# Half of the gated head outputs turned by transposing transfers instead of TensorE

## The chip, the cores and the metric

The kernel runs on one core of a Trainium2 chip. The metric is the device time of one execution in microseconds (us), as the median of several runs. In the tables PE is TensorE, PEld its weight loads, DVE is VectorE, ACT ScalarE, POOL GpSimd, and SP the SyncE queue that issues most loads. A tile has 128 partitions (P = 128).

## The reference

One decoder layer works on 512 tokens of 1024 channels in float32. Its two token mixers stand side by side: a convolution module, and a gated linear attention with four heads of 256 output channels. The change lies at the end of the attention:

```python
o = _gla_chunked(qh, kh, vh, gkh)                       # (1, 512, 4 heads, 256)
o = o * lax.rsqrt(jnp.mean(o * o, axis=-1, keepdims=True) + EPS) * gla_norm_g[l]
o = o.reshape(bsz, seq, GLA_VDIM) * jax.nn.silu(r)      # r is a product of the layer's input
y_gla = o @ w_gla_out[l]                                # (512, 1024) @ (1024, 1024)
merged = jax.nn.sigmoid(gate_a) * y_conv + jax.nn.sigmoid(gate_b) * y_gla
h = h + merged @ w_o[l]
```

A gated feed-forward block and a last normalization follow. The result is the (512, 1024) output.

## The kernel before

All large products are split into high and low parts: a float32 operand is copied on ACT into a rounded high part (`hi`), DVE subtracts it from the original to give the low part (`lo`), and `mm3` (L537 to L543) adds three products, low by high, high by low, high by high. So each weight tile of 128 x 1024 passes SP (load into `raw`), ACT (cast to `whi`) and DVE (subtract to `wlo`) ahead of PE. `split_weight` (L414) does that two weights ahead of the product that uses them (`LOOK = 2`).

A planner puts the instructions of each engine and of SP's queue in an order by their readiness and their place in the program text; each engine then works through its own list in order. `tc.issue_after(x)` pins what stands in its block behind `x` on the same engine.

The attention leaves its normalized outputs in `ot[p, n]`: token tile p (0 to 3, 128 tokens on partitions), column half n (512 of the 1024 channels). The product with `w_r` runs next, as a seven-product scheme over 2 x 2 blocks (`seven`, L1453). Its blocks come out in the order (token tiles 0 and 1, n = 0), (0 and 1, n = 1), (2 and 3, n = 1), (2 and 3, n = 0). `put_r` (L1544) evicts them into `rt[t, n]`, takes the SiLU on ACT, and lets DVE multiply the block finished before into `ot` (L1561); the last one is multiplied at L1565.

The product with `w_gla` needs channels on partitions. `gated_o(m)` (L1246) turns channel tile m (128 channels): four TensorE transposes (L1250), one for each token tile, into one PSUM bank of 512 tokens, which ACT scales by the norm's gain into the high part (L1257), and from which DVE makes the low part (L1258); the pair is `oa[m]`. Channel tiles 4 to 7 come from n = 1 and 0 to 3 from n = 0. `r_at` calls it for 4 and 5 during the last step of `w_r`. `pair_7(0)` calls it for 6, 7, then 0, 1, then 2, 3 after the first three of the four parts of its product pair with `w_gb` (`two_tiles`, L1344: parts x1, x3, x2, x4, each of some 24 products of 256 columns). Behind that pair stand the `w_gla` tiles 0 and 1 on PE, which read `oa[0]` to `oa[7]` in order, and then the pairs with `w_ga`.

In `two_tiles` a bank that a product adds to again is first copied out by ACT (`put`, L1351). POOL makes sums of weights (L398), pinned behind the instructions in `behind`.

Of the kernel before, what the change touches and what calls it, by code (L numbers as in the profile page):

```python
# [10 lines left out]
F32 = mybir.dt.float32  # L11
F32R = mybir.dt.float32r
BF16 = mybir.dt.bfloat16
U8 = mybir.dt.uint8
AF = mybir.ActivationFunctionType
ALU = mybir.AluOpType

P = 128
# [82 lines left out]
def trunk_layer(ctx: ExitStack, tc: tile.TileContext, a: dict, out: bass.AP):  # L101
    nc = tc.nc

    def pool(name, bufs, space=None):
        kw = {"space": space} if space is not None else {}
        return ctx.enter_context(tc.tile_pool(name=name, bufs=bufs, **kw))
# [9 lines left out]
    up = pool("acts", 1)  # L116
    tp = pool("temps", 1)
    ps = pool("psum", 1, bass.MemoryType.PSUM)
    edge = ctx.enter_context(tc.tile_pool(name="edge", bufs=1, side="right"))
    heap_scope, hp = scoped("heap", 26)  # L120
    conv_scope, vp = scoped("conv", 10)
# [5 lines left out]
    def nm(s):  # L127
        return f"{s}_{next(names)}"

    def heap(dt=F32):  # L130
        return hp.tile([P, T], dt, tag="h", name=nm("h"))
# [144 lines left out]
    pair_raws = {}  # L276
    kept = {}
    used = [0]
    pace = [None]

    def load():
        if len(raws) < len(order):
# [131 lines left out]
    def split_weight(halves=False, between=None):  # L414

        if len(ready) < len(order):
            while len(raws) <= len(ready):
                load()
            raw = raws[len(ready)]
            name, spec = order[len(ready)]  # L420
            if name in SEVEN or name == "two":
                raw = operand(raw, *spec) if name in SEVEN else two_operand(*spec)
                n = raw.shape[-1]
                hi = wp.tile([P, D], F32R, tag="whi", name=nm("whi"), bufs=4)[:, :n]
                lo = wp.tile([P, D], F32R, tag="wlo", name=nm("wlo"), bufs=4)[:, :n]
                nc.scalar.copy(hi, raw)  # L426
                two_low[:] = [nc.vector.tensor_tensor(lo, raw, hi.bitcast(F32), ALU.subtract)]  # L427
                with ExitStack() as order_of:
                    for ins in behind:
                        order_of.enter_context(tc.issue_after(ins.ins))  # L430
                    sum_on(name, *spec) if name in SEVEN else two_sums(*spec)
                ready.append((hi, lo))
                refill()
                return
            hi = wp.tile([P, D], F32R, tag="whi", name=nm("whi"), bufs=4)
            if order[len(ready)][0] == "w_low":
                nc.scalar.copy(hi, raw)
                if order[len(ready)][1] == 0:
                    part_lo = lambda t: t.rearrange("p (k c) -> p k c", c=P)[:, :, :RANK]
# [16 lines left out]
            nc.scalar.copy(hi, raw)  # L456
            if (name, spec) in ADDED:
                pace[0] = nc.scalar.mul(lo, raw, -1.0)  # L458
                nc.gpsimd.dma_start(lo, a[name][spec], accum_op=ALU.add)
            elif (name, spec) in POOLED:  # L460
                for c in (slice(0, T), slice(T, D)):
                    pace[0] = nc.gpsimd.tensor_tensor(lo[:, c], raw[:, c], hi[:, c].bitcast(F32), ALU.subtract)
            else:
                pace[0] = nc.vector.tensor_tensor(lo, raw, hi.bitcast(F32), ALU.subtract)  # L464
            ready.append((hi, lo))
            refill()

# [775 lines left out]

    ot = {}

    def gated_o(m, bank):  # L1246
        po = bank()
        c = (m % 4) * P
        for p in range(NT):
            nc.tensor.transpose(po[:, p * P : (p + 1) * P], ot[p, m // 4][:, c : c + P], ident)  # L1250
        gain = pp[:, PP_GG + m % 2 : PP_GG + m % 2 + 1]
# [4 lines left out]
        hi, lo = (both[:, 0, :], both[:, 1, :]) if m < 4 else (heap(F32R), heap(F32R))  # L1256
        nc.scalar.activation(hi, po, AF.Copy, scale=gain)  # L1257
        low_at[:] = [nc.vector.scalar_tensor_tensor(lo, po, gain, hi.bitcast(F32), ALU.mult, ALU.subtract)]  # L1258
        oa[m] = hi, lo

    part = [None] * KT

# [79 lines left out]
    combined = []  # L1342

    def two_tiles(name, p, q, acts7, side_bank, at_once=False):  # L1344

        x, y, z = mm_bank(), side_bank(), side_bank()
        c1, c2 = tmp(), tmp()
        t1, t2 = slice(0, H), slice(H, T)

        def put(c, acc):  # L1350
            nc.scalar.copy(c, acc[:, :H])  # L1351

        def combine(c, l, r, op):
            combined[:] = [nc.vector.tensor_tensor(c, l, r, op)]
# [185 lines left out]
    def sums_for(step):  # L1540
        while urgent and step in ("s1", "n2", "s4", "n3") and step not in merge_acts:
            urgent.pop(0)[1]()

    def put_r(step, t, n, acc):  # L1544
        if step in ("a11", "s1", "n2"):
            rt[t, n] = rp_.tile([P, T], F32, tag="r", name=nm("r"), bufs=6)
            return nc.scalar.copy(rt[t, n], acc)
        if step == "a22":
            rt[t, n] = rp_.tile([P, T], F32, tag="r", name=nm("r"), bufs=6)
            nc.scalar.activation(rt[t, n], acc, AF.Silu)  # L1550
        else:
            r = rt[t, n]
            one, two = (r, acc) if step == "n3" else (acc, r)
            done = nc.vector.tensor_tensor(r, one, two, ALU.add if step == "a12" else ALU.subtract)
            nc.scalar.activation(r, r, AF.Silu)
        if step == "a22":
            done = None
        with tc.issue_after(done.ins) if done else ExitStack():
            while gated:
                i, j = gated.pop()  # L1560
                nc.vector.tensor_tensor(ot[i, j], ot[i, j], rt[i, j], ALU.mult)  # L1561
        gated.append((t, n))
        if (step, t, n) == ("a22", 3, 0):
            i, j = gated.pop()
            nc.vector.tensor_tensor(ot[i, j], ot[i, j], rt[i, j], ALU.mult)  # L1565
        return done if step == "n3" else None

    def r_at(step, i):
        if (step, i) == ("a22", 1):
            for m in range(4, 6):  # L1570
                gated_o(m, ax_bank)

    seven("w_r", R_PAIRS, [ByTile(k) for k in range(4)], None, r_at, put=put_r, before=sums_for)
    half_of = [range(KT // 2), range(KT // 2, KT)]
    open_tiles = {}

# [2 lines left out]
    def pair_7(n):  # L1579
# [5 lines left out]
        for j in range(4):  # L1585
# [4 lines left out]
                while len(after) > 1:  # L1590
                    fill(1)
            if n == 0 and j < 3:
                for m in ((6, 7), (0, 1), (2, 3))[j]:
                    gated_o(m, ax_bank)
                if j == 2:
                    start_norms()
            if j == 0 or n >= 2:
# [424 lines left out]
```

## Time and profile before

| what | value |
|---|---|
| median of 3 runs | 817.36 us (817.26 to 817.85) |
| the profiled execution, its own time | 816.96 us |
| its span | 815.3 us |
| PE busy | 807.5 us (99%) |
| DVE busy | 700.7 us (86%) |
| ACT busy | 487.9 us (60%) |
| transposes of L1250 | 32, first at 284.2 us, last at 296.2 us |

The span is the time from the first to the last instruction that the profile shows; the execution's own time is 1.7 us longer. In the timeline a row has the start, the duration, the engine, the line, the operation with its tiles, and in brackets the idle time before it with what ended it. PE's matmuls overlap, so what one costs in the stream is read from the starts, not from its duration. Tiles carry the name of their buffers: `h` is the heap, `oa` the pair of channel tiles 0 to 3, `ax`, `mm` and `cv` are PSUM banks.

### The profile page before, as it was taken

To read this page: it belongs to the slowest core of one execution; us is meant where nothing else is said; L and a number is where in the kernel's file an instruction comes from. 1 tells how busy PE (TensorE), PEld (TensorE's weight loads), DVE (VectorE), ACT (ScalarE), POOL (GpSimd) and SP (SyncE) were. 2 spreads that over 40 slices of the span, in tenths; PEclk is the share of its full clock that TensorE was granted. 3 is DMA by queue.
4 is the path that set the end of the run, shared out by engine and by line. 5 is a ranking of instruction groups with operands and counts; after the bars stand their busy time and mean duration, and the time that the engine had idled before them with its cause. 6 is when DMAs were issued, how large, how long until landed. Compare 5 with 4: busy or idle time off the path is not lost.

```text
span 815.3 us, 11441 instructions
## 1 busy us (share of the span) xinstructions
PE 807.5 (99%) x4215; PEld 693.2 (85%) x4215; DVE 700.7 (86%) x1108; ACT 487.9 (60%) x746; POOL 192.5 (24%) x166
## 2 busy tenths in 40 slices
PE   9999999999999999999999999999999999999996
PEld 7888888788888898989888898898889988899885
DVE  6679999998998988486779899979976999789896
ACT  6667788677546575494435655556435663466655
POOL 2025433332204332122001100320133300522010
PEclk9999999999999999999999999999999999999999
DMA  8487858745831232432458613145732345334662
GB/s 337 146 198 179 187 160 176 161 119 135 186 95 60 78 130 78 137 105 95 164 124 220 190 57 126 52 154 156 144 127 92 142 117 167 105 104 171 165 129 105
DMA packets 36616, 113.60 MB, mean 139 GB/s; under 512 B 3704, under 2 KB 8960, under 8 KB 36560
## 3 DMA queue, kind: packets, MB, share of 16 engines
q1 hardware_dynamic: 29200, 86.92, 30.8%
q0 software_dynamic: 7200, 25.69, 18.0%
q8 instruction: 33, 0.54, 0.3%
q14 instruction: 23, 0.19, 0.1%
q10 hardware_dynamic: 160, 0.27, 0.1%
HBM read 110.76 MB, written 2.10 MB: 138 GB/s over the span
## 4 chain that ended last, share of the span: by engine, by line
PE 84%; DVE 13%; issue 1%; ACT 1%; DMA 1%; SPq 0%; DVEq 0%; ACTq 0%
PE mm L541 20%; PE mm L542 20%; PE mm L543 20%; DVE c L902 5%; PE cv L541 4%; PE cv L542 4%; PE cv L543 4%; DVE aside L902 3%; PE ax L542 2%; PE ax L541 2%; PE ax L543 2%; PE ax L1230 1%; PE ax L1232 1%; DMA kept<-in_w_r_dram 1%; PE ax L1212 0%
## 5 line engine op out<-in xcount | busy, mean ns | idle before, releaser
L541 PE MATMUL mm<-uh,wlo 128*128 128x512 f32 (+1 forms) x532 | 193.9, 364 | 0.2 <-DVE wlo L464 0.2
L542 PE MATMUL mm<-ul,whi 128*128 128x512 f32 (+1 forms) x532 | 191.6, 360 | 0.0
L543 PE MATMUL mm<-uh,whi 128*128 128x512 f32 (+1 forms) x532 | 191.4, 360 | 0.0
L427 DVE TENSOR_TENSOR wlo<-raw,whi 128x1024 fp32r<-128x1024 f32 x82 | 96.0, 1178 | 36.0 <-ACT whi L426 32.2
L398 POOL TENSOR_TENSOR raw<-raw,raw 128x512 f32<-128x512 f32 x39 | 63.9, 1638 | 236.3 <-DVE wlo L427 130.9
L541 PEld LDWEIGHTS mm<-uh,wlo 128*128 128x128 f32 x532 | 100.5, 189 | 15.6 <-DVE wlo L464 0.6
L543 PEld LDWEIGHTS mm<-uh,whi 128*128 128x128 f32 x532 | 100.4, 189 | 15.4
L542 PEld LDWEIGHTS mm<-ul,whi 128*128 128x128 f32 x532 | 100.5, 189 | 14.7
L426 ACT CAST whi<-raw 128x1024 fp32r<-128x1024 f32 x82 | 78.9, 965 | 41.4 <-PE mm L543 24.4
L456 ACT CAST whi<-raw 128x1024 fp32r<-128x1024 f32 x80 | 83.5, 1048 | 27.5 <-PE mm L543 13.9
L464 DVE TENSOR_TENSOR wlo<-raw,whi 128x1024 fp32r<-128x1024 f32 x50 | 66.3, 1331 | 7.1 <-ACT whi L456 6.8
L426 ACT CAST whi<-kept 128x1024 fp32r<-128x1024 f32 (+1 forms) x40 | 40.1, 1008 | 32.4 <-DVE kept L374 16.5
L902 DVE SCALAR_TENSOR_TENSOR aside<-cv,pp,aside 128x255 f32<-128x255 f32 (+6 forms) x112 | 52.2, 466 | 0.0
L902 DVE SCALAR_TENSOR_TENSOR c<-aside,btmp,c 128x247 f32<-128x247 f32 (+13 forms) x93 | 52.1, 565 | 0.0
L427 DVE TENSOR_TENSOR wlo<-kept,whi 128x1024 fp32r<-128x1024 f32 (+1 forms) x40 | 47.5, 1191 | 4.9 <-ACT whi L426 4.7
L902 DVE SCALAR_TENSOR_TENSOR c<-cv,pp,c 128x247 f32<-128x247 f32 (+13 forms) x93 | 43.2, 465 | 1.4 <-ACT c L898 1.4
L458 ACT ACTIVATE wlo<-raw 128x1024 fp32r<-128x1024 f32 x28 | 29.4, 1059 | 19.1 <-PE mm L541 19.1
L1351 ACT COPY tmp<-mm 128x256 f32<-128x256 f32 x38 | 14.1, 370 | 35.1 <-PE mm L543 34.3
L1733 DVE SCALAR_TENSOR_TENSOR tmp<-mm,pp,tmp 128x511 f32<-128x511 f32 (+1 forms) x42 | 31.2, 743 | 3.5 <-ACT tmp L1730 3.4
L1733 DVE SCALAR_TENSOR_TENSOR tmp<-tmp,pp,tmp 128x511 f32<-128x511 f32 (+1 forms) x32 | 27.8, 888 | 0.3
L1504 DVE TENSOR_TENSOR hres<-hres,mm 128x512 f32<-128x512 f32 (+1 forms) x37 | 24.7, 676 | 2.2 <-PE mm L543 2.1
L542 PE MATMUL cv<-ul,whi 128*128 128x512 f32 (+1 forms) x72 | 25.6, 356 | 0.0
(514 smaller groups left out, 2078.3 us busy)
## 6 DMA issues: line engine op xcount, KB each, us to landing
raw<-in_w_up_dram SPq DMA_DIRECT2D x44, 512.0 KB, 3.2
raw<-in_w_glu_dram SPq DMA_DIRECT2D x16, 512.0 KB, 5.1
raw<-in_w_down_dram SPq DMA_DIRECT2D x16, 512.0 KB, 3.4
wlo<-in_w_glu_dram POOLq DMA_DIRECT2D x12, 512.0 KB, 7.1
kept<-in_w_down_dram POOLq DMA_DIRECT2D x9, 512.0 KB, 5.5
raw<-in_w_v_dram SPq DMA_DIRECT2D x8, 512.0 KB, 6.0
raw<-in_w_qk_dram SPq DMA_DIRECT2D x8, 512.0 KB, 6.3
raw<-in_w_gb_dram SPq DMA_DIRECT2D x8, 512.0 KB, 4.0
```

The source lines that it names most:

```text
L398: work = nc.gpsimd.tensor_tensor(out, x, y, ALU.add)
L426: nc.scalar.copy(hi, raw)
L427: two_low[:] = [nc.vector.tensor_tensor(lo, raw, hi.bitcast(F32), ALU.subtract)]
L456: nc.scalar.copy(hi, raw)
L458: pace[0] = nc.scalar.mul(lo, raw, -1.0)
L464: pace[0] = nc.vector.tensor_tensor(lo, raw, hi.bitcast(F32), ALU.subtract)
L541: nc.tensor.matmul(acc, ll, rh, start=first, stop=False, **kw)
L542: nc.tensor.matmul(acc, lh, rl, start=False, stop=False, **kw)
L543: nc.tensor.matmul(acc, lh, rh, start=False, stop=last, **kw)
L902: nc.vector.scalar_tensor_tensor(out[:, j:], x[:, : half_t - j], w, out[:, j:], ALU.mult, ALU.add)
L1504: done = nc.vector.tensor_tensor(hres[t, n][:, c], hres[t, n][:, c], acc[:, c], op)
L1733: nc.vector.scalar_tensor_tensor(z[:, s:], acc[:, : T - s], w[j], z[:, s:], ALU.mult, ALU.add)
```

## The change

Token tiles 0 and 1 are turned by transfers, tiles 2 and 3 still by TensorE. After a block of tile 0 or 1 is gated, `words` has ACT reorder its float32 values into two planes of 16-bit words (all low words of a token, then all high ones), in the buffer of the SiLU tile that is no longer used, and SP writes them to DRAM, two rows for each token. When both tiles of a column half are written, `turn_o(n)` reads them back by transposing transfers, so that channels lie on partitions and the two words of a value beside each other again: one transfer of 512 rows by 512 words for n = 0, two of 512 by 256 for n = 1.

`gated_two` takes two channel tiles: for each two transposes into a bank of its own, and the high and low parts in halves of 256 tokens (`half_o`): the lower half from the landed tile, the upper one from the bank. The order on ACT and DVE is pinned: lower halves of 0 to 3 behind the last `put`, upper halves behind the last SiLU, lower halves of 4 to 7 behind the upper halves of 0 to 3, the next splits of `w_ga` and of `w_gla` tile 2 behind these, and the splits of `w_gb` behind the last reordering.

```diff
+    def words(t, n):
+        planes = rt[t, n].bitcast(U16).rearrange("p (two c) -> p two c", two=2)
+        behind_planes[:] = [nc.scalar.copy(planes, ot[t, n].bitcast(U16).rearrange("p (c two) -> p two c", two=2))]
+        rows = words_of[n][2 * t * P : 2 * (t + 1) * P, :]
+        nc.sync.dma_start(rows.rearrange("(p two) c -> p two c", two=2), planes)
+
+    def turn_o(n):
+        if n == 0:
+            landings = [rp_.tile([P, 4, H], F32, tag="rx", name=nm("turned"), bufs=1)]
+        else:
+            landings = [rp_.tile([P, 2, H], F32, tag="r", name=nm("turned"), bufs=6) for _ in range(2)]
+        many = 4 // len(landings)
+        for i, landing in enumerate(landings):
+            c = slice(i * many * P, (i + 1) * many * P)
+            nc.sync.dma_start(landing.bitcast(U16), words_of[n][:, c], transpose=True)
+            for j in range(many):
+                turned[4 * n + i * many + j] = landing[:, j, :]
+
+    def gated_two(m, bank):
+        for j in range(2):
+            po, c = bank(), (m % 4 + j) * P
+            for p in (2, 3):
+                nc.tensor.transpose(po[:, (p - 2) * P : (p - 1) * P], ot[p, m // 4][:, c : c + P], ident)
+            start_o(m + j)
+            if m < 4:
+                half_o(m + j, slice(0, H), turned[m + j], copied, ())
+            late_halves[:] = half_o(m + j, slice(H, T), po[:, :H], last_silu, ())
+        if m < 4:
+            low_at[:] = late_halves[1:]
+            for j in range(2):
+                behind_halves[:] = half_o(m + 4 + j, slice(0, H), turned[m + 4 + j], late_halves[:1], late_halves[1:])
+
+    def half_o(m, c, x, behind_high, behind_low):
+        (hi, lo), gain = oa[m], pp[:, PP_GG + m % 2 : PP_GG + m % 2 + 1]
+        with following(behind_high):
+            high = nc.scalar.activation(hi[:, c], x, AF.Copy, scale=gain)
+        with following(behind_low):
+            return high, nc.vector.scalar_tensor_tensor(lo[:, c], x, gain, hi[:, c].bitcast(F32), ALU.mult, ALU.subtract)
...
+                late = behind_halves if spec[0] == "w_ga" else ()
+                with following(late[:1] or (behind_planes if spec[0] == "w_gb" else ())):
+                    nc.scalar.copy(hi, raw)
+                with following(late[1:]):
+                    two_low[:] = [nc.vector.tensor_tensor(lo, raw, hi.bitcast(F32), ALU.subtract)]
...
+    def gate_o(t, n):
+        nc.vector.tensor_tensor(ot[t, n], ot[t, n], rt[t, n], ALU.mult)
+        if t < 2:
+            words(t, n)
+        if t == 1:
+            turn_o(n)
...
         if (step, t, n) == ("a22", 3, 0):
-            i, j = gated.pop()
-            nc.vector.tensor_tensor(ot[i, j], ot[i, j], rt[i, j], ALU.mult)
+            gate_o(*gated.pop())
+            gated_two(4, ax_bank)
...
-                for m in ((6, 7), (0, 1), (2, 3))[j]:
-                    gated_o(m, ax_bank)
+                gated_two((6, 0, 2)[j], ax_bank)
```

`following` is `tc.issue_after` of the first instruction of its list, or nothing where the list is empty. `last_silu` is the last SiLU of `put_r`, `copied` the last `put`.

More of the change, by code (lines that the diff above doesn't have):

```diff
@@ L14 @@
 U8 = mybir.dt.uint8
+U16 = mybir.dt.uint16
 AF = mybir.ActivationFunctionType
@@ L118, in trunk_layer @@
     ps = pool("psum", 1, bass.MemoryType.PSUM)
+    dram = pool("dram", 1, bass.MemoryType.DRAM)
     edge = ctx.enter_context(tc.tile_pool(name="edge", bufs=1, side="right"))
@@ L275, in trunk_layer @@
     ready, raws = [], []
-    pair_raws = {}
+    pair_raws, behind_planes, behind_halves = {}, [], []
     kept = {}
@@ L279, in trunk_layer, with following @@
     pace = [None]
+    def following(ops):
+        return tc.issue_after(ops[0].ins) if ops else ExitStack()
     def load():
@@ L425, in split_weight @@
                 lo = wp.tile([P, D], F32R, tag="wlo", name=nm("wlo"), bufs=4)[:, :n]
-                nc.scalar.copy(hi, raw)
-                two_low[:] = [nc.vector.tensor_tensor(lo, raw, hi.bitcast(F32), ALU.subtract)]
+                late = behind_halves if spec[0] == "w_ga" else ()
[3 more added lines that the diff above has]
+                    two_low[:] = [nc.vector.tensor_tensor(lo, raw, hi.bitcast(F32), ALU.subtract)]
                 with ExitStack() as order_of:
@@ L455, in split_weight @@
                 return [[lambda c=c, part=part: part(c) for c in cols] for part in (high, low)]
-            nc.scalar.copy(hi, raw)
+            late = behind_halves if (name, spec) == ("w_gla", 2) else ()
+            with following(late[:1]):
+                nc.scalar.copy(hi, raw)
             if (name, spec) in ADDED:
@@ L463, in split_weight @@
             else:
-                pace[0] = nc.vector.tensor_tensor(lo, raw, hi.bitcast(F32), ALU.subtract)
+                with following(late[1:]):
+                    pace[0] = nc.vector.tensor_tensor(lo, raw, hi.bitcast(F32), ALU.subtract)
             ready.append((hi, lo))
@@ L1244, in trunk_layer, with start_o @@
     ot = {}
[L1246 to L1251, printed above, removed]
+    last_silu, late_halves = [], []
+    turned, words_of = {}, [dram.tile([T, DV * 2], U16, name=nm("words")) for _ in range(2)]
+    def words(t, n):
[27 more added lines that the diff above has]
+                behind_halves[:] = half_o(m + 4 + j, slice(0, H), turned[m + 4 + j], late_halves[:1], late_halves[1:])
+    def start_o(m):
         if m < 3:
@@ L1255, in gated_o @@
             both = tp.tile([P, 2, T], F32R, tag="gain", name=nm("oa"), bufs=1)
[L1256 to L1259, printed above, removed]
+        oa[m] = (both[:, 0, :], both[:, 1, :]) if m < 4 else (heap(F32R), heap(F32R))
+    def half_o(m, c, x, behind_high, behind_low):
[4 more added lines that the diff above has]
+            return high, nc.vector.scalar_tensor_tensor(lo[:, c], x, gain, hi[:, c].bitcast(F32), ALU.mult, ALU.subtract)
     part = [None] * KT
@@ L1340, in step_of_two @@
             mm3(acc[:, :H], (w[0][:, s], w[1][:, s]), (ah[k], al[k]), opens and k == 0, k == 3, not opens)
-    combined = []
+    combined, copied = [], []
     def two_tiles(name, p, q, acts7, side_bank, at_once=False):
@@ L1350, in put @@
         def put(c, acc):
-            nc.scalar.copy(c, acc[:, :H])
+            copied[:] = [nc.scalar.copy(c, acc[:, :H])]
         def combine(c, l, r, op):
@@ L1549, in put_r @@
             rt[t, n] = rp_.tile([P, T], F32, tag="r", name=nm("r"), bufs=6)
-            nc.scalar.activation(rt[t, n], acc, AF.Silu)
+            last_silu[:] = [nc.scalar.activation(rt[t, n], acc, AF.Silu)]
         else:
@@ L1559, in put_r @@
             while gated:
-                i, j = gated.pop()
-                nc.vector.tensor_tensor(ot[i, j], ot[i, j], rt[i, j], ALU.mult)
+                gate_o(*gated.pop())
         gated.append((t, n))
         if (step, t, n) == ("a22", 3, 0):
-            i, j = gated.pop()
-            nc.vector.tensor_tensor(ot[i, j], ot[i, j], rt[i, j], ALU.mult)
+            gate_o(*gated.pop())
+            gated_two(4, ax_bank)
         return done if step == "n3" else None
-    def r_at(step, i):
-        if (step, i) == ("a22", 1):
-            for m in range(4, 6):
-                gated_o(m, ax_bank)
-    seven("w_r", R_PAIRS, [ByTile(k) for k in range(4)], None, r_at, put=put_r, before=sums_for)
+    seven("w_r", R_PAIRS, [ByTile(k) for k in range(4)], None, put=put_r, before=sums_for)
     half_of = [range(KT // 2), range(KT // 2, KT)]
@@ L1592, in pair_7 @@
             if n == 0 and j < 3:
-                for m in ((6, 7), (0, 1), (2, 3))[j]:
-                    gated_o(m, ax_bank)
+                gated_two((6, 0, 2)[j], ax_bank)
                 if j == 2:
```

## The prediction

> **What bounds the kernel now.** I read the page first, then the waits of PE, then the timeline of PE around the turning of the head outputs, and only then the engines and queues that feed that place.
>
> ```profile
> span 815.3 us, 11441 instructions
> PE 807.5 (99%) x4215; PEld 693.2 (85%) x4215; DVE 700.7 (86%) x1108; ACT 487.9 (60%) x746; POOL 192.5 (24%) x166
> ...
> PE mm L661 <- DVE ones L634: 1.1, 1, 1.1
> PE mm L541 <- DVE wlo L464: 0.2, 1, 0.2
> ```
>
> PE is busy 807.5 of 815.3 us, and the view of PE's waits holds 1.3 us in all. So time goes only where PE gets less to do or a wait becomes larger than what hides it. The clock is no term: page and stages show it fully granted.
>
> The change touches PE through the transposes of L1250. The first row below groups them, the others are one of their four blocks in PE's timeline (start, duration).
>
> ```profile
> L1250 PE MATMUL ax<-ident,h x32: 270/272/273, 284.2 to 296.2; 128*128 128x128 f32 x32
> ...
> 287.80 0.28 PE L543 MATMUL mm<-uh,whi 128*128 128x256 f32 x1
> 287.92 1.04 PE L1250 MATMUL ax<-ident,h 128*128 128x128 f32 x8
> 288.71 0.36 PE L541 MATMUL mm<-hq,wlo 128*128 128x256 f32 x1
> 288.91 0.28 PE L542 MATMUL mm<-hq,whi 128*128 128x256 f32 x1
> 289.03 0.28 PE L543 MATMUL mm<-hq,whi 128*128 128x256 f32 x1
> ```
>
> One transpose lasts 0.272 us, but they overlap: the eight start at 287.92 and the next product at 288.71, so each takes 0.79 / 8 = 0.099 us of PE's stream. The product behind the block takes 0.20 instead of the usual 0.12 (288.91 to 289.03), 0.08 us per block.
>
> **The change, part by part.** *Removed:* 16 of 32 transposes, those of token tiles 0 and 1. Four blocks stay, with four transposes each, and so do their four tails of 0.08. Gain on PE: 16 x 0.099 = **1.58 us**. By the duration it would be 16 x 0.272 = 4.35; I take the pitch, because the next product starts by it. The Trainium skill (TensorE: Matmul & The Clock Gate, Part 4: PE-mode transpose) gives about 275 ns for one transpose in a kernel's context. The trace agrees on the duration (272), but a sum by it, 4.4 us, is not what 32 of them take here (4 x 0.79 = 3.2 us).
>
> *Added on ACT:* four reorderings of a gated tile into two planes of 16-bit words (1024 elements in, 1024 out). No row shows one; between a plain 512-element copy (0.57) and twice the 1024-element cast (2 x 1.05). I take 1.05, since the element count is the cast's.
>
> ```profile
> 260.06 0.57 ACT L1547 COPY r<-mm 128x512 f32<-128x512 f32 x1
> ...
> 279.05 1.99 ACT L426 CAST whi<-raw 128x1024 fp32r<-128x1024 f32 x2
> ...
> 283.14 1.05 ACT L426 CAST whi<-raw 128x1024 fp32r<-128x1024 f32 x1 [0.89 <-PE mm L543]
> ...
> core 0: us, PE busy (x) PEld busy (x) DVE busy (x) ACT busy (x) POOL busy (x), PEclk, DMA share, GB/s
> 255.00:278.00 23.00, 23.00 (x103) 19.07 (x102) 21.56 (x20) 12.76 (x16) 8.68 (x5) 1.00 0.20 69
> 278.00:284.00 6.00, 5.88 (x27) 4.57 (x26) 5.75 (x8) 4.51 (x6) 1.37 (x1) 1.00 0.00 0
> 284.00:298.00 14.00, 14.00 (x120) 13.87 (x119) 11.29 (x15) 10.75 (x19) 1.52 (x2) 1.00 0.47 152
> ```
>
> Three fall into 255 to 278, where ACT is free for 10.2 us. The fourth, of tile (1,1), comes about 279.1, and the new order puts the w_gb casts of 279.05 behind it: 1.05 later on ACT. Behind ACT stand DVE's low halves of those weights, done at 280.20 + 2.35 = 282.55 (rows below); the first product needs its low half at 284.96 in the old clock, 284.56 after one shortened block, and only the first of the two. So 2 us of cover against 1.05 (2.1 at the upper end): nothing, and 0.1 to 0.5 us if all goes badly.
>
> *Moved and split:* each channel tile's high and low part is made in two pieces of 256 tokens. A 256-column ACT copy is 0.37, two of 512 columns are 1.26: 8 x (0.74 - 0.63) = 0.9 us more on ACT. DVE's nearest 256-column operation is 0.41, its two of 512 are 1.41: 8 x (0.82 - 0.70) = 1.0 us more. In 284 to 298 ACT has 3.25 us free and DVE 2.7. In the old order the last pieces (298.21) queued behind two weight splits on DVE; the new one puts those splits behind the pieces, and their products come only after both w_gla tiles, past 308. So the last pieces come earlier than now, not later.
>
> ```profile
> 280.20 2.35 DVE L427 TENSOR_TENSOR wlo<-raw,whi 128x1024 fp32r<-128x1024 f32 x2
> ...
> 284.96 0.36 PE L541 MATMUL mm<-uh,wlo 128*128 128x256 f32 x1
> ...
> 291.86 0.37 ACT L1351 COPY tmp<-cv 128x256 f32<-128x256 f32 x1 [0.55 <-PE cv L543]
> ...
> 293.80 1.41 DVE L1258 SCALAR_TENSOR_TENSOR oa<-ax,pp,oa 128x512 fp32r<-128x512 f32 x2 [2.06 <-ACT oa L1257]
> 295.13 0.41 DVE L1354 TENSOR_TENSOR tmp<-tmp,mm 128x256 f32<-128x256 f32 x1
> ...
> 296.55 1.26 ACT L1257 ACTIVATE oa<-ax,pp 128x512 fp32r<-128x512 f32 x2
> ...
> 298.21 1.41 DVE L1258 SCALAR_TENSOR_TENSOR oa<-ax,pp,oa 128x512 fp32r<-128x512 f32 x2
> ```
>
> *Added on SP:* four writes of 256 KB, then one transposing transfer of 512 KB and two of 256 KB that read them back. Their first transposing one waits for two writes to land, and everything later on SP's queue stands behind that wait.
>
> ```profile
> 271.00 1.81 DVE L1561 TENSOR_TENSOR h<-h,r 128x512 f32<-128x512 f32 x1
> ...
> 278.40 0.68 DVE L1561 TENSOR_TENSOR h<-h,r 128x512 f32<-128x512 f32 x1
> ...
> 270.49 14.76 SPq L296 DMA_DIRECT2D raw<-in_w_gla_dram  x2
> 286.01 2.19 SPq L292 DMA_DIRECT2D raw<-in_w_ga_dram  x2
> ...
> wlo<-in_w_gb_dram POOLq DMA_DIRECT2D x6, 512.0 KB, 8.9
> raw<-in_w_gla_dram SPq DMA_DIRECT2D x8, 512.0 KB, 3.7
> raw<-in_w_down_dram SPq DMA_DIRECT2D x4, 256.0 KB, 2.7
> out_dram<-hres SPq DMA_DIRECT2D x2, 256.0 KB, 2.0
> ```
>
> Columns n = 0: the second gating ends at 272.81, the plane is made by 274 to 275, the write lands 2.0 later, at 277. Columns n = 1: 279.08, 280.2, 282.2. No row shows a transposing transfer. Lower end: it lands like a plain load, 3.7 us for 512 KB and 2.7 for 256 KB. A slower row of that size is 8.9. Far end: it moves in pieces of 256 bytes (the 128 words that make one column of a landing), each taking what a mean packet of the SP queue takes:
>
> ```profile
> q1 hardware_dynamic: 29200, 86.92, 30.8%
> ```
>
> 0.308 x 16 x 815.3 / 29200 = 0.138 us; 512 KB are 2048 pieces, 128 per DMA engine, 17.6 us. I take 3.7 to 8.9, nearest in size: landed at 281 to 286 (n = 0) and at 285 to 291 (n = 1, two of up to 4.5 in series). They are read first behind the copy of 291.86, and the n = 1 pieces behind the upper halves of channel tiles 0 and 1, whose transposes start at 291 (now 291.66). Hidden, then, with 0 to 10 us in hand. SP's plain loads behind it: the second w_gla tile (issued 284.9 now) would go out perhaps 2 us later, to be cast at 292; its product is due past 302. Nothing.
>
> When PE needs the pieces, from PE's timeline and the groups by tile (oa is channel tiles 0 to 3, h is 4 to 7):
>
> ```profile
> 297.70 0.40 PE L541 MATMUL mm<-oa,wlo 128*128 128x512 f32 x1
> ...
> L541 PE MATMUL mm<-h,wlo x8: 389/389/389, 300.4 to 307.9; 128*128 128x512 f32 x8
> ```
>
> Channel tile 0 is due at 297.70, 4 at 300.4, 6 at 300.4 + 6 x 0.23 = 301.8; 1.58 earlier after the change, so 6 is due at 300.2.
>
> **Sum.** The profiled execution's own time is 816.96 (span 815.3, 1.7 around it); less 1.58 it is 815.4. The median of the runs is 817.36, 0.4 higher: 817.36 - 1.58 = **815.8 us**. About 0.2% of 817.36, 1.63 us, is what a measurement here tells from no change, so the forecast lies on that bound (815.73).
>
> **Rivals.** *A bubble goes with it.* At the start of the last step PE idles for a bank that DVE reads late:
>
> ```profile
> 278.12 0.39 PE L543 MATMUL mm<-whi,sumsq 128*128 128x512 f32 x1
> 278.62 0.47 PE L541 MATMUL cv<-whi,ul 128*128 128x512 f32 x1
> ...
> 277.80 0.68 DVE L1554 TENSOR_TENSOR r<-r,cv 128x512 f32<-128x512 f32 x1
> ```
>
> 0.50 between starts instead of 0.23, 0.27 us lost, because the bank's reader stands behind a weight split on DVE. ACT's new copies reshuffle that stretch. For it: the planner works it out anew; against: DVE is full there (21.56 of 23) and gains nothing. Price: 817.36 - 1.85 = 815.5.
>
> *The gain is eaten on SP and ACT.* SP sat for a buffer between the two w_gla loads (270.49, and 14.76 to the end of the second). If the write of tile (1,0), ready at 274, stands behind the second one in SP's queue, it lands only at 285.25 + 2.0 = 287.3. The tile's buffer is due for the last SiLU tile, which ACT writes at 284.37 now; ACT would stand still until 287.3, and with it the copy of 286.68, which PE needs before the product of 288.71 (then 287.9) adds to the same bank:
>
> ```profile
> 284.37 0.60 ACT L1550 ACTIVATE r<-mm 128x512 f32<-128x512 f32 x1 [0.18 <-PE mm L543]
> ...
> 286.68 0.37 ACT L1351 COPY tmp<-mm 128x256 f32<-128x256 f32 x1
> ```
>
> SiLU, cast, pieces and copy behind 287.3 reach 289 to 290: PE loses 1 to 2 us, 816.8 to 817.8, say 817.3. Against: the order of a queue is planned by when its items are ready.
>
> *Slower: transposing is slow.* By the far end, n = 0 lands at 277 + 17.6 = 294.6, then two of 8.8 in series, the last at 312.2; 0.37 + 0.41 for the pieces, 313.0 against the 300.2 at which PE needs channel tile 6: 12.8 us, 815.8 + 12.8 = 828.6. It decides once the last landing comes after 299.4, that is once the three need over 22 us together. The Trainium skill (VectorE: DVE Perf Modes, The three transpose paths) speaks for it: 1309 ns for one 128x128 two-byte tile by DMA, and advice to use TensorE where PSUM will do. By an estimate from that page 32 such tiles in series are 42 us, last landing at 319, some 835. No run here shows that operation yet. Against: 16 DMA engines share a transfer in every row above.
>
> **Chances.** Forecast 0.52; bubble gone 0.19; eaten 0.12; slow transposing 0.17. The forecast's own range, 815.2 to 816.4, falls half on each side of 815.73: faster by over 0.2% is 0.19 + 0.26 = 0.45, within 0.2% 0.26 + 0.12 = 0.38, slower 0.17. The range from 815.0 (bubble and 0.5 more) to 819.0 (eaten, and the first of slow transposing) leaves out most of the last case and little else.
>
> **What would show it.** Right: L1250 x16, its blocks taking 0.40 us of PE; a start of the first w_gla product about 1.6 earlier; the landings before 291; PE's waits still near 1.3 us. Wrong: a wait of ACT on the landed tiles, or of PE on the pieces of L1258's successor; SP held at a transposing issue past 290; casts of w_gb late enough that PE waits at 284.6; and a planner's order after 300 that opens new gaps on PE.

## The result, and the profile after

The changed kernel takes 816.01 us (median of 15 runs, 815.21 to 816.62) against 817.36 us before (15 runs, 816.88 to 818.03): a ratio of 0.9982, 95% interval 0.9974 to 0.9990. That is 1.35 us faster where 1.58 was forecast. The profiled execution's own time is 815.44 us.

From the page of the changed kernel the busy times, and then from its view of PE's waits (who waits, for whom; total us, times, longest):

```profile
PE 805.6 (99%) x4199; PEld 690.8 (85%) x4199; DVE 702.9 (86%) x1116; ACT 492.6 (61%) x758; POOL 189.4 (23%) x166
```

```profile
PE cv L553 <- DVE r L1608: 0.3, 1, 0.3
...
PE ax L1284 <- DVE h L1306: 0.2, 1, 0.2
```

PE has 16 instructions fewer, ACT twelve more (four planes and eight more pieces), DVE eight more. Two of PE's waits stand at the place of the change: one for the bank `cv` at the start of the last step of `w_r` (before, the view lists none there, though the starts show 0.27 us lost), and a new one for a bank `ax` in the middle of a block of transposes. Both stand in PE's timeline after (start, duration, and in brackets the idle time with what ended it):

```profile
277.80 0.39 PE L555 MATMUL mm<-whi,sumsq 128*128 128x512 f32 x1
278.49 0.47 PE L553 MATMUL cv<-whi,ul 128*128 128x512 f32 x1 [0.30 <-DVE r L1608]
...
287.32 0.38 PE L1284 MATMUL ax<-ident,h 128*128 128x128 f32 x2
287.86 0.44 PE L1284 MATMUL ax<-ident,h 128*128 128x128 f32 x2 [0.16 <-DVE h L1306]
288.06 0.36 PE L553 MATMUL mm<-hq,wlo 128*128 128x256 f32 x1
...
291.02 0.60 PE L1284 MATMUL ax<-ident,h 128*128 128x128 f32 x4
291.37 0.36 PE L553 MATMUL mm<-sumsq,wlo 128*128 128x256 f32 x1
...
296.43 0.40 PE L554 MATMUL mm<-oa,whi 128*128 128x512 f32 x1
```

For the last place, PE's timeline before:

```profile
297.93 0.40 PE L542 MATMUL mm<-oa,whi 128*128 128x512 f32 x1
```

An undisturbed block took 0.79 us of PE and takes 0.35 now (291.02 to 291.37): 0.44 saved. The block of 287.32 waits in its middle and takes 0.74. The starts of equal products, before and after:

| place on PE | before | after | difference |
|---|---|---|---|
| last product ahead of the last step of w_r | 278.12 | 277.80 | -0.32 |
| first product of that step | 278.62 | 278.49 | -0.13 |
| behind the first block of transposes | 284.96 | 284.38 | -0.58 |
| behind the second | 288.71 | 288.06 | -0.65 |
| behind the third | 292.45 | 291.37 | -1.08 |
| a high product of w_gla, behind the fourth | 297.93 | 296.43 | -1.50 |

The -0.32 is no work of the change: products at 32 us, far ahead of it, already start 0.42 earlier in this execution, and in the profiled executions of this study that last product starts anywhere from 277.64 to 278.80. From the first row to the last the change gains 1.18 us: four blocks by 0.44 are 1.76; the longer gap at 278 takes 0.19 back, and the second block 0.38.

The transfers end in time. First ACT's groups by line (count, busy, mean ns), then the rows of the landed tiles by the view of that tile, then SP's timeline, all after:

```profile
L1264 ACT COPY r<-h 128x1024 uint16<-128x1024 uint16 x4 | 4.2, 1046 | 1.0 <-DVE h L1592 1.0
```

```profile
L1304 ACT ACTIVATE oa<-turned,pp x4: 506/508/512, 291.5 to 294.2; 128x256 fp32r<-128x256 f32 x4
...
L1304 ACT ACTIVATE h<-turned,pp x4: 509/514/517, 293.0 to 296.7; 128x256 fp32r<-128x256 f32 x4
...
L1276 SPq DMA_TRANSPOSE turned<-words x3: 1231/1246/2349, 275.5 to 283.4; - x3
...
DMA to landing us min/median/max: 3.6/3.9/4.6
```

```profile
273.50 0.34 SPq L1266 DMA_DIRECT2D words<-r  x1
275.51 2.35 SPq L1276 DMA_TRANSPOSE turned<-words  x1
...
282.10 2.58 SPq L1276 DMA_TRANSPOSE turned<-words  x2
```

The first (n = 0) lands 4.6 after 275.51, at 280.1, the last (issued at 283.4) by 288; the pieces of the one are read from 291.5 on, those of the other from 293.0. The load behind them goes out at 285.76, 0.9 later than before, and PE does not wait for it.

### The profile page after: what moved, and what is told of

It is laid out like the page before. It is cut to its first block, busy times and chain, and to the rows that moved or that the text cites. A ratio compares the mean times of both kernels' runs of the same rounds, so it can differ in the third digit from the quotient of the medians.

```text
span 813.6 us, 11446 instructions
## 1 busy us (share of the span) xinstructions
PE 805.6 (99%) x4199; PEld 690.8 (85%) x4199; DVE 702.9 (86%) x1116; ACT 492.6 (61%) x758; POOL 189.4 (23%) x166
## 4 chain that ended last, share of the span: by engine, by line
PE 83%; DVE 14%; issue 1%; ACT 1%; DMA 1%; SPq 0%; DVEq 0%; ACTq 0%
PE mm L553 19%; PE mm L554 19%; PE mm L555 19%; DVE c L914 5%; PE cv L554 4%; PE cv L553 4%; PE cv L555 4%; DVE aside L914 3%; PE ax L555 2%; PE ax L553 2%; PE ax L554 2%; PE mm L770 1%; DVE wlo L436 1%; PE ax L1242 1%; PE ax L1244 1%
## 5 line engine op out<-in xcount | busy, mean ns | idle before, releaser
L404 POOL TENSOR_TENSOR raw<-raw,raw 128x512 f32<-128x512 f32 x39 | 61.9, 1588 | 238.7 <-DVE wlo L436 122.1
```

What stands on the lines that cost most here:

```text
L404: work = nc.gpsimd.tensor_tensor(out, x, y, ALU.add)
```

## The experiments

Each kernel below is the changed kernel with the edit shown. The kernel before took 817.28 to 817.35 us beside these runs; a ratio is to it, with its 95% interval.

### All transposes back on TensorE

```diff
-        if t < 2:
-            words(t, n)
-        if t == 1:
-            turn_o(n)
...
-            for p in (2, 3):
-                nc.tensor.transpose(po[:, (p - 2) * P : (p - 1) * P], ot[p, m // 4][:, c : c + P], ident)
+            for p in range(NT):
+                nc.tensor.transpose(po[:, p * P : (p + 1) * P], ot[p, m // 4][:, c : c + P], ident)
...
+            half_o(m + j, slice(0, H), po[:, :H], last_silu, ())
+            late_halves[:] = half_o(m + j, slice(H, T), po[:, H:], last_silu, ())
```

> The changed kernel with all 32 transposes on PE again and no reordering, write or transposing transfer; channel tiles still evicted in halves of 256 tokens, splits still pinned behind them. My theory, that the gain is PE's stream and nothing else: 16 x 0.099 = 1.58 us come back, 817.0 to 817.8, within 0.3 us of before. Rival, that the halves and the set order of the splits bring (or cost) something by themselves: more than 0.5 us away from before, so 816.0 to 816.8, or over 818.

Measured: 818.56 us (817.90 to 819.05), 1.0015 (1.0006 to 1.0024), slower than before. What is left of the change here, the pieces and the set order (a bank for each channel tile was there before), is not neutral as I had thought: it costs 1.2 us. Against this kernel the turning by transfers is worth 2.5 us. From PE's waits and timeline in this kernel:

```profile
PE ax L1284 <- DVE h L1304: 0.4, 1, 0.4
```

```profile
293.04 0.63 PE L1284 MATMUL ax<-ident,h 128*128 128x128 f32 x4 [0.44 <-DVE h L1304]
```

The gap at `cv` is there again (before, 0.27 beyond the pitch; here 0.44, from 278.31 to 278.98). The wait for a bank is not that of the changed kernel: it stands in the third block, which takes 1.43 (292.00 to 293.43) instead of 0.79, while the second block is undisturbed (0.80). By the starts the two explain 0.17 + 0.64 of the 1.2; where the rest lies I did not find.

### No turning at all

```diff
-        if t < 2:
-            words(t, n)
-        if t == 1:
-            turn_o(n)
+        if (t, n) in ((1, 0), (1, 1)):
+            for k in range(4):
+                turned[4 * n + k] = ot[t, n][:, :H]
```

> The changed kernel without the reorderings, the writes and the transposing transfers; the lower halves read an unturned gated tile, so the turning of token tiles 0 and 1 is left out of the computation. It shows what the 16 transposes left out of PE are worth with nothing in their place. Theory, that the transfers are fully hidden and only the ACT reorderings move DVE's order before the last step of w_r: the wait there (0.46 us after against 0.28 before) falls back, so 0.2 to 0.3 us faster than the changed kernel, 815.6 to 815.9. Rival, that the transfers or the wait on the landings cost PE time: 1 us or more faster than the changed kernel, under 815.1.

Measured: 815.92 us (815.03 to 816.17), 0.9982 (0.9973 to 0.9991). The changed kernel has 816.01: by the medians, planes, writes and transposing transfers cost nothing that can be measured. The trace shows a little more. DVE's and PE's timelines of this kernel around the second block:

```profile
280.44 2.35 DVE L436 TENSOR_TENSOR wlo<-raw,whi 128x1024 fp32r<-128x1024 f32 x2
...
286.77 0.47 DVE L1306 SCALAR_TENSOR_TENSOR h<-ax,pp,h 128x256 fp32r<-128x256 f32 x1
```

```profile
287.70 0.60 PE L1284 MATMUL ax<-ident,h 128*128 128x128 f32 x4
288.06 0.36 PE L553 MATMUL mm<-hq,wlo 128*128 128x256 f32 x1
```

The wait for `ax` is gone: the second block takes 0.36, not 0.74. From the last product ahead of the last step of `w_r` to the high product behind the fourth block PE takes 18.24 us (278.19 to 296.43), and 18.63 in the changed kernel (277.80 to 296.43). So that wait of some 0.4 us comes with the turning by transfers; by which path is told further down. It is smaller than the scatter of the executions, and the medians do not show it.

I had also expected the gap at `cv` to shrink without the planes on ACT. It did not:

```profile
PE cv L553 <- DVE r L1607: 0.3, 1, 0.3
```

So the planes are not its cause.

### Each transposing transfer issued twice, and four times

```diff
-            nc.sync.dma_start(landing.bitcast(U16), words_of[n][:, c], transpose=True)
+            for _ in range(2):
+                nc.sync.dma_start(landing.bitcast(U16), words_of[n][:, c], transpose=True)
```

> The changed kernel with each of the three transposing transfers issued twice in succession into the same landing, so that the turned tiles land about twice as late after their writes. Theory, that the landings have time in hand until PE needs channel tile 6 near 299: the column half n = 0 lands near 285, n = 1 near 293 to 295, the second w_gla weight is loaded some 6 us later (near 292) and still in time; 815.8 to 816.6. Rival, that what hides the transfers is used up already (landed pieces stand at the head of ACT's queue at 291.5): 2 us or more slower, 818 or above.

> The changed kernel with each transposing transfer issued four times in succession into the same landing. By the price of the slow-transposing rival, PE stalls by the last landing plus 0.8 less 299 to 300: four times 4.6 us from 275.5 for n = 0, then two writes and eight transfers in series of some 3 to 4 us, last landing between 312 and 325, so 13 to 25 us slower, 829 to 841. Rival, that even this is hidden, or that the transfers of SP overlap: under 822.

Measured: twice, 815.66 us (815.05 to 816.05), 0.9979 (0.9970 to 0.9988), hidden as forecast, a little under the range that I gave. Four times, 822.65 us (822.39 to 822.95), 1.0065 (1.0051 to 1.0079): neither number holds. SP's timeline with four of each:

```profile
280.82 15.93 SPq L1277 DMA_TRANSPOSE turned<-words  x9
```

The nine in one row follow each other at 15.93 / 9 = 1.77 us on average, though each lands 3.8 to 6.2 us after its issue: a repeated transfer does not wait for the one before to land, which I had reckoned with. So the time is below the forecast. The stall itself begins earlier than I had placed it. ACT's timeline of this kernel, and PE's waits:

```profile
291.61 0.37 ACT L1399 COPY tmp<-cv 128x256 f32<-128x256 f32 x1 [0.17 <-PE cv L555]
296.83 0.51 ACT L1305 ACTIVATE oa<-turned,pp 128x256 fp32r<-128x256 f32 x1 [4.85 <-DMA turned<-words]
```

```profile
PE ax L1285 <- DVE oa L1307: 3.2, 1, 3.2
```

ACT works in its order. It stands at the first lower piece from 291.98 on, and the upper pieces behind it, which free the banks of the transposes, stand with it. PE waits for a bank (3.2 us), long before it needs channel tile 6.

### One bank for a pair of channel tiles

```diff
-        for j in range(2):
-            po, c = bank(), (m % 4 + j) * P
-            for p in (2, 3):
-                nc.tensor.transpose(po[:, (p - 2) * P : (p - 1) * P], ot[p, m // 4][:, c : c + P], ident)
+        both = bank()
+        for j in range(2):
+            for p in (2, 3):
+                c = (m % 4 + j) * P
+                to = both[:, j * H + (p - 2) * P : j * H + (p - 1) * P]
+                nc.tensor.transpose(to, ot[p, m // 4][:, c : c + P], ident)
+        for j in range(2):
+            po = both[:, j * H :]
```

> The changed kernel with one PSUM bank for the two channel tiles of a pair (four transposes into four quarters, then the evictions) instead of a bank each. Theory, that PE's 0.33 us in the second block is a wait for a bank that DVE reads late, three banks for four tiles: it goes, 0.3 us faster, 815.6 to 815.8. Rival, that sharing a bank makes the evictions of the pair wait for each other or for PE and DVE's next work comes later: same or up to 1 us slower, 816 to 817.

Measured: 815.81 us (815.04 to 816.26), 0.9980 (0.9971 to 0.9989). The wait for `ax` is gone from PE's waits, and the one for `cv` stays. So the second block has to wait for the late read only as long as each channel tile takes a bank of its own. But most of what this saves goes into another pause, too short for the view of waits. DVE's and PE's timelines of this kernel, later:

```profile
296.73 1.22 DVE L476 TENSOR_TENSOR wlo<-raw,whi 128x1024 fp32r<-128x1024 f32 x1
297.86 0.47 DVE L1310 SCALAR_TENSOR_TENSOR oa<-ax,pp,oa 128x256 fp32r<-128x256 f32 x1
```

```profile
298.01 0.39 PE L553 MATMUL mm<-oa,wlo 128*128 128x512 f32 x1
298.39 0.50 PE L554 MATMUL mm<-oa,whi 128*128 128x512 f32 x1
```

The last piece of channel tile 2 stands behind a split of `w_gla` on DVE and ends at 298.33; the product that reads it starts 0.38 after the one ahead of it and the next (298.73) 0.34 later, instead of 0.23 each: 0.26 lost. The rival, that DVE's work comes later, held in part. The 0.2 us between the two kernels' medians is not larger than their scatter.

### The order not set

```diff
     def following(ops):
-        return tc.issue_after(ops[0].ins) if ops else ExitStack()
+        return ExitStack()
```

> The changed kernel without any of the set orders between the halves, the reorderings and the next weight splits; the planner alone decides. Theory, that the pieces have 1.6 us less time than before since PE comes earlier, and that before the last one was ready only some 0.4 us ahead of its product: with two weight splits ahead of them again PE stalls by 1 us or so, 816.6 to 817.6, near before. Rival, that the pins do nothing: 815.8 to 816.3.

Measured: 816.63 us (816.21 to 817.00), 0.9991 (0.9982 to 1.0000), within the forecast, but not by the stall that I had put there. From PE's waits of this kernel, then DVE's timeline:

```profile
PE ax L1284 <- DVE h L1306: 0.9, 1, 0.9
```

```profile
284.31 2.32 DVE L1306 SCALAR_TENSOR_TENSOR oa<-turned,pp,oa 128x256 fp32r<-128x256 f32 x3
...
288.89 0.47 DVE L1306 SCALAR_TENSOR_TENSOR h<-ax,pp,h 128x256 fp32r<-128x256 f32 x1
```

Without the order DVE takes three lower pieces of `oa` as soon as they have landed, and the piece that frees the bank of channel tile 4 comes at 288.89 (287.34 in the changed kernel; counted from the last product ahead of the last step, 10.44 against 9.54). Against the 816.01 and 815.76 us of the changed kernel the set order is worth 0.6 to 0.9, by keeping early pieces out of the way of a bank.

### The low half of one weight later, with one bank

Beside the edit of the bank, the low half of the last weight of `w_r` is taken by DVE behind its read of the step's bank, not ahead of it:

```diff
+                def low():
+                    two_low[:] = [nc.vector.tensor_tensor(lo, raw, hi.bitcast(F32), ALU.subtract)]
+                if name == "w_r" and spec[1:] == ("a22", 1):
+                    later_low.append(low)
+                else:
+                    with following(late[1:]):
+                        low()
...
         with tc.issue_after(done.ins) if done else ExitStack():
+            while later_low:
+                later_low.pop()()
             while gated:
```

> The changed kernel with one bank for a pair of channel tiles, and with the low half of w_r's last weight put behind DVE's read of the bank that the last step of w_r opens. Theory, that the 0.46 us before that step come from DVE's order (a 1.2 us subtraction that took 2.3 us beside POOL's sum stood ahead of the read): both waits go, 0.7 to 0.8 us faster than the changed kernel, 815.1 to 815.5. Rival, that the wait moves to the low half itself or to the next weights: 815.8 to 816.8.

Measured: 815.45 us (814.91 to 815.78), 0.9976 (0.9966 to 0.9985). Of the waits only the 1.1 us at the start of the program is left in PE's list. PE's and DVE's timelines of this kernel at the place:

```profile
278.80 0.39 PE L561 MATMUL mm<-whi,sumsq 128*128 128x512 f32 x1
279.03 0.39 PE L559 MATMUL cv<-whi,ul 128*128 128x512 f32 x1
```

```profile
276.50 0.69 DVE L1618 TENSOR_TENSOR r<-r,cv 128x512 f32<-128x512 f32 x1
277.11 1.63 DVE L436 TENSOR_TENSOR wlo<-kept,whi 128x1024 fp32r<-128x1024 f32 x1
```

The read of `cv` comes first, the subtraction behind it, and PE goes on at its usual 0.23. So the subtraction ahead of that read makes the gap. The kernel before has the same order in its rows, but was not run with this edit. The pause ahead of the last piece of channel tile 2 is here too (298.19 comes 0.53 after 297.66, the next product 0.34 later: 0.41 lost). Against the changed kernel the trace thus gives 0.46 at `cv` and 0.38 at `ax`, less 0.41: 0.43.

Then the changed kernel and this one again, on one chip:

> The changed kernel itself, on the chip of the two kernels beside it, for a comparison at one place: 815.7 to 816.3.

> One bank for a pair and the low half of w_r's last weight behind the bank's read, once more beside the changed kernel. Theory, that the two waits of 0.46 and 0.33 us are really gone: 0.5 to 0.8 us below the changed kernel of this call. Rival, that the difference of 815.45 to 816.01 was scatter between calls: within 0.3 us of it.

Measured: 815.76 us (815.51 to 816.22), 0.9982 (0.9973 to 0.9990), and 815.35 us (814.84 to 816.11), 0.9977 (0.9967 to 0.9986). It is the fastest kernel found, twice some 1.9 us under the one before; its 0.4 us under the changed kernel is a little less than forecast and agrees with the 0.43 of the trace, but with these scatters the medians alone do not settle it.

### A whole column half turned by transfers

Tokens 2 and 3 of n = 1 are turned by transfers too, so that two of the four blocks go:

```diff
-        if t < 2:
+        if t < 2 or n == 1:
             words(t, n)
-        if t == 1:
-            turn_o(n)
+        if (t, n) in ((1, 0), (1, 1), (3, 1)):
+            turn_o(n + t // 2)
...
-            gated_two(4, ax_bank)
...
-                gated_two((6, 0, 2)[j], ax_bank)
+                if j:
+                    gated_two((6, 0, 2)[j], ax_bank)
```

> All of the column half n = 1 (channel tiles 4 to 7, token tiles 0 to 3) by transfers: two more reorderings on ACT, two more writes, two more transposing transfers of 256 KB; two of the four transpose blocks are gone. Theory, PE's stream decides as long as landings come before 299: 8 x 0.099 + 2 x 0.08 = 0.95 us and the bank wait of 0.33 us gone, 1.2 to 1.3 us faster than the changed kernel, 814.7 to 815.0. Rival, that ACT, already dense between 278 and 285, is delayed by two more copies of 1.05 us so that weights or bank reads come late: same as the changed kernel or slower, 816 to 818.

Measured: 816.60 us (815.84 to 816.95), 0.9989 (0.9980 to 0.9998). The rival held: eight transposes less on PE, and 0.6 us slower than the changed kernel. ACT's timeline and PE's waits:

```profile
293.64 1.31 ACT L1307 ACTIVATE h<-turned,pp 128x256 fp32r<-128x256 f32 x3 [0.73 <-DMA turned<-words]
```

```profile
PE mm L553 <- ACT tmp L1401: 0.5, 1, 0.5
PE mm L553 <- DVE tmp L1404: 0.5, 1, 0.5
```

The first of these waits ends at 287.40, behind a copy of a bank that ACT makes after a late cast of `w_gb`; the second at 295.86, behind a sum that DVE takes only after the three pieces that waited for a landing.

In two further versions the landed tiles of these tokens have buffers of their own, their pieces come last on ACT and DVE, and the later low half of above is added. In the second the pieces are in the order in which PE reads them and ahead of a sum of L1079:

```diff
+            for k in range(4, 8) if m == 2 else ():
+                behind_halves[:] = half_o(k, slice(H, T), turned[k + 4], behind_halves[:1], behind_halves[1:])
```

```diff
+            for k, c in ((4, early), (5, early)) if m == 0 else ((4, late), (5, late), (6, early), (6, late), (7, early), (7, late)):
+                behind_halves[:] = half_o(k, c, turned[k if c == early else k + 4], behind_halves[:1], behind_halves[1:])
+            low_at[:] = behind_halves[1:]
```

> All of n = 1 by transfers as in the kernel more_turns, but with the two late landings in the heap instead of the SiLU tiles' buffers, the lower pieces of channel tiles 0 and 1 free to go as soon as they have landed, the late pieces last, and the low half of w_r's last weight behind the bank's read. Theory, that more_turns lost its 1.2 us to a SiLU tile that waited 5.7 us for a buffer and to pieces that stood ahead of bank reads: PE's stream gets 0.95 us shorter and no wait replaces it, 814.5 to 815.2. Rival, that DVE has no room left for the pieces between 291 and 299: 815.5 to 816.8.

> As more_spread, with the late pieces of channel tiles 4 to 7 in the order in which PE reads them and ahead of the first step of the convolution's normalization on DVE. Theory, that the 2.8 us for which PE waited on a late piece in more_spread come from DVE's order alone (a split and a 1.8 us step stood ahead of five pieces): 2.3 to 2.8 us faster than more_spread, 815.5 to 816.1, or below if nothing replaces the wait. Rival, that DVE between 284 and 299 has not the time for the pieces in any order: within 1 us of 818.3.

Measured: 818.34 us (816.81 to 820.09), 1.0012 (1.0003 to 1.0021), and 816.01 us (815.18 to 817.26), 0.9984 (0.9975 to 0.9993). DVE's timeline of the first, then of the second:

```profile
296.67 1.77 DVE L1079 TENSOR_TENSOR sum<-btmp,sum 128x512 fp32r<-128x512 f32 x1
298.36 3.06 DVE L1317 SCALAR_TENSOR_TENSOR h<-turned,pp,h 128x256 fp32r<-128x256 f32 x5
```

```profile
296.05 5.50 DVE L1319 SCALAR_TENSOR_TENSOR h<-turned,pp,h 128x256 fp32r<-128x256 f32 x6
```

In the first PE waits 2.8 us for these pieces, in the second 0.8: the order of the pieces decided over some 2.3 us. But the six pieces of the second take 0.92 us each (5.50 / 6), beside POOL's sums of weights (295.93 to 300.09), and PE's waits still hold 0.8 us for them. What eight more transposes saved went into a wait for DVE.

## Why the prediction was right, and where it was not

**The removed term** was right in kind and a little small: 1.58 by the pitch. An undisturbed block of four takes 0.35, not the 0.40 of the pitch, so it gave 0.44, which is 1.76 for four blocks. The sum by the durations, 4.35, no run came near.

**The planes on ACT** cost 1046 ns each (1.05 estimated), and PE never waited for a split of `w_gb`. That was all that the prediction asked of this term before it put it at nothing, and there its working failed: what stands on DVE behind those splits comes later with them. ACT's timeline after, from the fourth plane on, and DVE's:

```profile
278.98 1.05 ACT L1264 COPY r<-h 128x1024 uint16<-128x1024 uint16 x1
279.93 1.05 ACT L434 CAST whi<-raw 128x1024 fp32r<-128x1024 f32 x1
```

```profile
281.01 1.23 DVE L436 TENSOR_TENSOR wlo<-raw,whi 128x1024 fp32r<-128x1024 f32 x1 [0.87 <-ACT whi L434]
...
284.49 2.32 DVE L436 TENSOR_TENSOR wlo<-raw,whi 128x1024 fp32r<-128x1024 f32 x1
...
287.34 0.47 DVE L1306 SCALAR_TENSOR_TENSOR h<-ax,pp,h 128x256 fp32r<-128x256 f32 x1
```

The read of the same bank in DVE's timeline before:

```profile
286.51 0.74 DVE L1258 SCALAR_TENSOR_TENSOR h<-ax,pp,h 128x512 fp32r<-128x512 f32 x1
```

DVE stands idle for 0.87 until the first cast behind the plane is done, and the read of channel tile 4's bank comes 9.54 after the last product ahead of the last step. Before it came 8.39 after that product, in the kernel without planes 8.58 (286.77), and with all transposes on TensorE, also without planes, 8.57 (286.88). PE reaches the second block 9.52 after that product, where it took 9.80 before. So the second block loses 0.38 of its 0.44, within the 0.1 to 0.5 that the prediction gave for the bad case. One bank for two tiles takes this wait away, and so does leaving out the turning.

**The bubble** at the start of the last step did not go; it grew, 0.50 to 0.69 between starts. DVE's timeline after, then before:

```profile
275.43 2.32 DVE L436 TENSOR_TENSOR wlo<-kept,whi 128x1024 fp32r<-128x1024 f32 x1
277.67 0.68 DVE L1608 TENSOR_TENSOR r<-r,cv 128x512 f32<-128x512 f32 x1
```

```profile
276.67 1.21 DVE L427 TENSOR_TENSOR wlo<-kept,whi 128x1024 fp32r<-128x1024 f32 x1
```

The subtraction ahead of the read of `cv` (before at 277.80) took 1.21 before and takes 2.32 now, beside a sum on POOL. It is not the planes (the kernel without them has it too); why POOL's sum falls there now is open. That the gap can go, with about 0.4 us, the kernel with the later low half shows. So the rival named a true reserve, and its condition, that a new order would by itself bring the read forward, was wrong.

**What is left.** 1.76 - 0.19 - 0.38 = 1.19 stands beside the 1.35 of the medians; the 0.16 between them is within the scatter of the executions. That the forecast of 815.8 lies so near 816.01 is in part luck: the removed term was 0.18 too small, and two losses of 0.57 together had been put at nothing.

**The pieces of 256 tokens and the set order** were put at nothing as well. The pieces took 0.47 to 0.51 on ACT and 0.47 on DVE, not 0.37 and 0.41, but in the changed kernel PE waits for none of them. What the pieces cost there by themselves no run shows; the set order is worth 0.6 to 0.9 there, and with all transposes on TensorE the two together cost 1.2.

**The gain eaten on SP and ACT** did not occur: the write of tile (1,0) went out at 273.50 and stood behind no w_gla load.

**Slow transposing** fell. The 512 KB landed 4.6 us after its issue, inside the 3.7 to 8.9 that I took, and far from 17.6. The Trainium skill (VectorE: DVE Perf Modes, The three transpose paths) gives 1309 ns for one tile of 128x128 two-byte words; this transfer holds 16 such tiles, 0.29 us each. The trace does not agree with a sum in series, and the measurement decides. A step of this rival was wrong as well: a landing costs time not only once it misses PE's need of channel tile 6 (299.4), but already once it misses the moment at which ACT, in its order, reaches the landed piece (291.5 for the first), as the kernel with four issues of each shows. The columns of n = 1 had landed by 288 and were read at 293.0: 5 us of cover, where 299.4 would leave 11.

## What to carry to other kernels

On an engine that never rests, price a removed operation by the pitch of its starts, and then look at every buffer that this engine now reaches earlier: its reader on another engine has to come as much earlier, or the gain turns into a wait. A copy put on another engine is not free because its next user stays in time: here the splits behind it were in time, and the read of a bank behind the splits was not. Work moved to a queue is hidden only up to the point at which some engine, working in its order, stands at the first landed piece, and that may be long before the data are needed. What a change brings along to make room for its main step, here pieces and a set order, has a price that is worth measuring by itself: 1.2 us in the kernel with all transposes on TensorE.

## What the runs showed of the hardware

**A DVE subtraction beside POOL.** The same subtraction of two 128x1024 tiles in SBUF took 1.22 us alone (289.05 in DVE's timeline after) and 2.32 beside a sum on POOL. POOL's timeline after:

```profile
274.92 1.74 POOL L404 TENSOR_TENSOR raw<-raw 128x512 f32<-128x512 f32 x1
284.05 1.68 POOL L404 TENSOR_TENSOR raw<-raw,raw 128x512 f32<-128x512 f32 x1 [7.39 <-DVE wlo L436]
```

Both slow subtractions (275.43 and 284.49) begin after such a sum has begun and end about one undisturbed duration after it: 276.66 + 1.09 and 285.73 + 1.08. The Trainium skill (SBUF — State Buffer, Who interferes with whom) says that a DVE instruction with two SBUF inputs contends with a GpSimd instruction that reads SBUF, that the ports they share are an exclusive lock, and that the order of issue decides who blocks. The trace agrees: the subtractions that begin behind the sum last until it has ended and their own time has passed. In the kernel without planes the later of the two sums runs from 282.87 to 284.55; there the subtraction (285.03) took 1.21, and the two multiplications of tiles in SBUF that stand ahead of it took 2.39 together, against 1.28 before. No run here moved POOL's sums by themselves.

**Transposing transfers.** In the changed kernel SP is taken for 2.35 us by the issue of 512 KB (1.92 to 2.22 in other kernels) and 1.23 to 1.25 by one of 256 KB, against 0.33 to 0.35 for most plain ones. They land 3.6 to 4.6 us after the issue, not far from plain loads of that queue (2.6 for 256 KB of `w_down`, 3.5 for 512 KB of `w_gla`), and repeated ones follow each other every 1.77 us on average. What they cost here is time in SP's queue.
